# Rows of the second norm made at the head of the mix, and the norm's products run in halves

## The chip, the core and the metric

The kernel runs on one core of one Trainium2 chip. The metric is the device time of one execution in microseconds (us). TensorE (PE) does the matmuls; VectorE (DVE), ScalarE (ACT) and GpSimd (POOL) work on rows of 128 partitions; SyncE (SP) issues the DMAs, in the order of one queue. Matmul results land in PSUM, everything else lies in SBUF.

## What is computed

One layer of an encoder runs for 384 tokens: 128 sample tokens (8 sequences of 16) and 256 prompt tokens. Two branches (an RWKV-7 time mixing and a sparse attention) are projected, gated and summed, then projected once more, and a norm and a feed-forward part with many small experts (PEER) follow:

```python
mod = jax.nn.silu(c) @ lp['w_ada'] + lp['b_ada']
sh1, sc1, g1, sh2, sc2, g2 = [m[:, None, :] for m in jnp.split(mod, 6, axis=-1)]
...
m = gate_a * (o_a @ lp['w_proj_a']) + gate_b * (o_b @ lp['w_proj_b'])
x = x + g1 * (m @ lp['w_out'])
h2 = _rmsnorm(x, lp['norm2_w']) * (1 + sc2) + sh2
x = x + g2 * _peer(h2, lp['w_pq'], lp['peer_keys'], lp['peer_u'], lp['peer_v'])
```

The change touches only how `g1`, `sc2`, `sh2` and `norm2_w` are brought to the tiles, and how the line of `h2` is worked out.

## The kernel before

The tokens form three tiles of 128 rows: tile 0 the samples, tiles 1 and 2 the prompt. Matmuls split each operand into a high and a low part (`hilo`, L228: the high part on ACT, the low part on DVE or POOL) and run three products of the parts.

`run` (L1577) goes through stages. In the front the RWKV and attention units run in an order written out by hand (`ORDER`, L177), with the modulation units (`mod_unit`, L383) and the gate units between them. A modulation unit stores its 256 columns of `mod` to a DRAM buffer. Then the pools of the front are closed, the pool of the mix is opened on their memory, and `mix` (L1168) projects the two branches. `parts` (L1159) loads a branch output from DRAM in four pieces (`px`, two buffers) and splits them into `pbh`/`pbl` (first branch) or `pah`/`pal` (second). For each of eight 128-column groups it loads a gate row (`ga` in the first branch, `gm` in the second), multiplies and sums, and splits the sum into `mT`, in the buffers `pbh` and `pbl` again.

After that loop `mix` makes three sets of rows by `modrow` (L407). It loads 1024 columns of `mod` from DRAM into the one buffer `modr`, then the bias row of the same columns into its row 9 (L412, a second DMA that writes into the same tile), and multiplies by a selecting matrix, once for each of two token groups and two column halves, so that each token has its row in PSUM (`fx`, two buffers). Row 2 (`g1`) is copied by ACT to `row2`, row 4 becomes (1 + scale) x norm weight on DVE in `pah`, with the norm weights loaded into the third part of that buffer (L1191), and row 3 (the shift) is copied to `pal`. The x rows of the three tiles are loaded (L1206) into the third part of `pal` and into `ga`.

`out_unit` (L1211, four times) projects `mT` by `w_out`, multiplies by `g1` on DVE (L1219, `tm` with two buffers) and adds to the x rows on POOL (L1220). `h2_tile` (L1222, three times) stores the new x rows, squares and sums them on ACT (L1229), takes the root on POOL (L429, in `rstd`), multiplies by the root and the scale on DVE (L1231), adds the shift (L1232), and transposes on PE in two groups of four (L1241). The tile `h2` (shown as `h`) has two buffers; tile 0 also stores it to DRAM (L1234). Tile 0's transposes are split for `scores_s`, those of tiles 1 and 2 go to `h2f`, which `scores_p` and the expert matmuls read. `peer_select` (L1279) then picks the experts, mostly on DVE.

The order of instructions on each engine isn't the traced one. A scheduler lays it out before the run from a simulated time (`schedule_with_timeline_sim`, L1727): each engine takes, of what is ready in that simulation, what was traced first. On the chip each engine, and the SP queue, then follows that fixed order. A pool that takes over the memory of closed pools is a boundary: its tiles wait for the last use in those pools.

Of the kernel before, what the change touches and what calls it, by code (L numbers as in the profile page):

```python
# [17 lines left out]
AF = mybir.ActivationFunctionType  # L18
OP = mybir.AluOpType
# [176 lines left out]
class K:  # L196
    def __init__(self, ctx, tc, I, O):
        self.ctx, self.tc, self.nc, self.I, self.O = ctx, tc, tc.nc, I, O
        self.uid = 0
        self.const = self.open(ctx, "const")  # L200
        self.stream = self.open(ctx, "stream")
        self.dram = self.open(ctx, "dram", space=bass.MemoryType.DRAM)
        self.nlo = 0
        self.lo_pattern = "v"
# [55 lines left out]
    def win_ap(self, name):  # L260
        n = UNITS[name][1]
        return self.I["w_in"][:, UOFF[name]:UOFF[name] + 8 * n].rearrange("p (k c) -> p k c", k=8)

# [30 lines left out]
    def load_consts(self, n, pool):  # L294
        arr, offs = PACKS[n]
        cp = pool.tile([128, arr.shape[1]], F32, name=n)
        self.nc.sync.dma_start(cp, self.I[n])
        for k, (o, shp) in offs.items():
# [7 lines left out]
    def setup(self):  # L306
# [4 lines left out]
        cols = self.fconst.tile([128, 91], F32, name="cols")  # L311
        nc.sync.dma_start(cols, self.I["cols"])
        o = 0
# [15 lines left out]
    def setup_front(self):  # L329
# [4 lines left out]
        rn = self.t([128, 128], tag="qkn")  # L334
        nc.sync.dma_start(rn, self.I["rows"][:, 5120:5248].to_broadcast([128, 128]))
        self.load_consts("clate", self.const)
# [831 lines left out]
    def mix(self):  # L1168
        nc = self.nc
        I = self.I  # L1170
        gb = self.t([128, 8, NT], tag="ga")
        for br, (src, w, tg) in enumerate(((self.oad, "w_proj_a", "pb"), (self.obd, "w_proj_b", "pa"))):
            LT = self.parts(src, tg)
            if br:
                mh, ml = self.mT = [self.t([128, 8, NT], F32R, tag=tag) for tag in ("pbh", "pbl")]
            for u in range(4):
                W = self.wload(I[w][:, u], 256)
                for c in range(2):
                    k = 2 * u + c
                    g = self.t([128, NT], tag="gm", bufs=2) if br else gb[:, k]  # L1180
                    nc.sync.dma_start(g, self.gd[8 * br + k])
                    p = self.tposp(W, c, 128, LT)
                    nc.vector.tensor_tensor(g, g, p, op=OP.mult)
                    if br:
                        nc.gpsimd.tensor_tensor(g, g, gb[:, k], op=OP.add)
                        self.hilo(mh[:, k], ml[:, k], g, eng="v")

        self.g1 = self.t([128, 2, 1024], tag="row2")
        an = self.t([128, 3, 1024], tag="pah")
        bx = self.t([128, 3, 1024], tag="pal")  # L1190
        nc.sync.dma_start(an[:, 2], I["rows"][:, 0:1024].to_broadcast([128, 1024]))  # L1191
        self.A2, self.B2 = an, bx
        for j in (2, 4, 3):
            pp = self.modrow(j)
            for sp in range(2):
                for b in range(2):
                    cols = slice(b * 512, b * 512 + 512)
                    if j == 4:
                        nc.vector.scalar_tensor_tensor(an[:, sp, cols], pp(sp, b), 1.0, an[:, 2, cols], op0=OP.add, op1=OP.mult)
                    else:  # L1200
                        nc.scalar.activation((self.g1 if j == 2 else bx)[:, sp, cols], pp(sp, b), AF.Copy)
        self.x1 = [bx[:, 2]]
        xr = self.t([128, 2, 1024], tag="ga")
        self.x1 += [xr[:, 0], xr[:, 1]]
        for i in range(3):
            nc.sync.dma_start(self.x1[i], I["x"][i * 128:(i + 1) * 128])  # L1206
        self.x1d = self.dt_([NT, 1024])
        self.h2d = self.dt_([128, 1024])
# [13 lines left out]
    def h2_tile(self, i):  # L1222

        nc = self.nc
        x1 = self.x1[i]
        nc.sync.dma_start(self.x1d[i * 128:(i + 1) * 128], x1)
        h2 = self.t([128, 1024], tag="h2", bufs=2)
        ss = self.t([128, 1], tag="ss", bufs=2)
        nc.scalar.activation(h2, x1, AF.Square, accum_out=ss)  # L1229
        r = self.rstd(ss, ss, 1.0 / 1024, EPS)  # L1230
        nc.vector.scalar_tensor_tensor(h2, x1, r, self.A2[:, min(i, 1)], op0=OP.mult, op1=OP.mult)  # L1231
        nc.vector.tensor_tensor(h2, h2, self.B2[:, min(i, 1)], op=OP.add)  # L1232
        if i == 0:
            nc.sync.dma_start(self.h2d, h2)  # L1234
        if i == 0:
            self.h2T = [self.t([128, 8, 128], F32R, tag="poh", bufs=2, pool=self.sel) for _ in "hl"]
        t0 = max(i - 1, 0) * 128
        for hb in range(2):
            p = self.ps([128, 4, 128], tag="fx")
            for c in range(4):  # L1240
                nc.tensor.transpose(p[:, c], h2[:, (hb * 4 + c) * 128:(hb * 4 + c + 1) * 128], self.ident)  # L1241
            hs = slice(hb * 4, hb * 4 + 4)
            o = (slice(None), hs, slice(t0, t0 + 128))
            if i == 0:
                self.hilo(self.h2T[0][o], self.h2T[1][o], p, eng="v")
            else:
                nc.scalar.activation(self.h2f[o], p, AF.Copy)
# [492 lines left out]
```

## Time and profile before

| | |
|---|---|
| median of 3 runs | 1787.35 us (1784.87 to 1787.41) |
| the profiled execution's own time | 1789.7 us |
| its span | 1787.9 us |
| mean PE clock granted | 0.978 |
| PE, DVE, ACT, POOL busy | 95%, 77%, 42%, 31% |
| mean DMA rate | 244 GB/s |

The page cuts the span into 40 slices of 44.7 us; a digit is the busy share in tenths:

```profile
PE   6999999999999998999999999999998989999998
DVE  4538787777867765455999998899957877888787
DMA  9443662454364365665498989975589989999995
```

The mix and the norm lie in slices 16 to 19 (about 708 to 850 us). Times in views are microseconds from the start of the span; "idle before" in brackets is how long an engine stood still ahead of an instruction, and what ended that. Durations of single instructions come from this one execution.

### The profile page before, as it was taken

What the parts mean: (1) busy time and instruction counts of PE and PEld (TensorE: products, weight loads), DVE (VectorE), ACT (ScalarE), POOL (GpSimd) and SP (SyncE); (2) the same over time, 40 slices, a digit from 0 to 9 for tenths busy, and PEclk for the clock granted to TensorE, in tenths of its full rate; (3) what the DMA queues carried; (4) which work ended last, traced back from release to release, by engine and by line L of the source; (5) the groups of instructions that cost most, each with busy time, mean ns of one, the idle gap of its engine ahead of it and who ended that gap; (6) DMA issues with size and microseconds to landing.
All of it is one profiled execution on the core that took longest, in us unless ns stands there. A gap on an engine that the chain in (4) does not pass through costs nothing.

```text
span 1787.9 us, 33229 instructions
## 1 busy us (share of the span) xinstructions
PE 1695.1 (95%) x12424; PEld 1414.2 (79%) x12424; DVE 1368.0 (77%) x2925; ACT 754.4 (42%) x1647; POOL 556.7 (31%) x648
## 2 busy tenths in 40 slices
PE   6999999999999998999999999999998989999998
PEld 4987788878888876998788789999976666666666
DVE  4538787777867765455999998899957877888787
ACT  4533333333243333334323365579833433334344
POOL 2423243333332320034032232333342324233232
PEclk8999899999999998999999999999999999999999
DMA  9443662454364365665498989975589989999995
GB/s 319 150 121 92 195 191 73 145 166 146 95 208 141 104 219 203 202 199 176 131 349 328 347 303 375 367 239 178 186 316 369 354 332 388 388 359 372 382 371 190
DMA packets 172537, 436.71 MB, mean 244 GB/s; under 512 B 46036, under 2 KB 86100, under 8 KB 155992
## 3 DMA queue, kind: packets, MB, share of 16 engines
q1 hardware_dynamic: 153944, 300.36, 49.9%
q0 software_dynamic: 18432, 134.23, 19.8%
q8 instruction: 98, 1.61, 0.4%
q14 instruction: 63, 0.52, 0.1%
HBM read 403.23 MB, written 31.30 MB: 243 GB/s over the span
## 4 chain that ended last, share of the span: by engine, by line
PE 55%; DVE 19%; DMA 13%; issue 7%; ACT 3%; POOL 2%; SPq 1%; DVEq 0%; POOLq 0%; ACTq 0%
PE mm L226 21%; PE fx L226 13%; PE dx L226 8%; PE cp L226 6%; PE bx L226 5%; DMA w<-in_pv 4%; DVE wl L234 3%; DMA w<-in_puT 3%; DVE raw L1567 3%; DVE acc L1573 2%; DMA raw<-in_puv,pe 2%; ACT wh L230 1%; DMA d<-MBp 1%; DMA NL<-d 1%; DMA w<-in_w_ada 1%
## 5 line engine op out<-in xcount | busy, mean ns | idle before, releaser
L234 DVE TENSOR_TENSOR wl<-w,wh 128x1024 fp32r<-128x1024 f32 (+1 forms) x280 | 352.8, 1265 | 121.2 <-ACT wh L230 80.2
L230 ACT ACTIVATE wh<-w 128x1024 fp32r<-128x1024 f32 (+1 forms) x288 | 301.1, 1052 | 195.0 <-PE mm L226 83.9
L1560 POOL DMA_INDIRECT raw<-in_puv,pe x128 | 169.3, 1323 | 438.8 <-PE dx L226 128.3
L226 PE MATMUL fx<-h2h,wl 128*128 128x256 f32 x736 | 210.5, 286 | 9.5 <-DVE wl L234 9.3
L226 PE MATMUL fx<-h2h,wh 128*128 128x256 f32 x736 | 212.9, 289 | 5.0 <-ACT wh L230 3.0
L226 PE MATMUL fx<-h2l,wh 128*128 128x256 f32 x736 | 207.6, 282 | 0.0
L1573 DVE SCALAR_TENSOR_TENSOR acc<-raw,dots,acc 128x1024 f32<-128x1024 f32 x127 | 166.5, 1311 | 18.3 <-ACT dots L1569 18.1
L1567 DVE SCALAR_TENSOR_TENSOR raw<-raw,sh 128x1024 f32<-128x1024 f32 x128 | 157.8, 1233 | 9.7 <-DMA raw<-in_puv,pe 9.6
L226 PEld LDWEIGHTS fx<-h2h,wl 128*128 128x128 f32 x736 | 138.4, 188 | 13.8 <-DVE wl L234 13.4
L226 PEld LDWEIGHTS fx<-h2h,wh 128*128 128x128 f32 x736 | 138.7, 188 | 9.3 <-ACT wh L230 5.0
L226 PEld LDWEIGHTS fx<-h2l,wh 128*128 128x128 f32 x736 | 138.7, 188 | 2.1 <-issue 1.6
L226 PE MATMUL fx<-h2f,w 128*128 128x256 f32 x576 | 131.1, 388 | 8.3 <-ACT G L1476 8.3
L226 PEld LDWEIGHTS fx<-h2f,w 128*128 128x128 f32 x576 | 110.6, 194 | 27.0 <-ACT G L1476 11.1
L226 PE MATMUL mm<-LTh,wh 128*128 128x384 f32 (+2 forms) x352 | 123.8, 352 | 2.0 <-ACT wh L230 1.4
L226 PE MATMUL mm<-LTl,wh 128*128 128x384 f32 (+2 forms) x352 | 123.1, 350 | 0.9 <-POOL LTl L481 0.9
L226 PE MATMUL mm<-LTh,wl 128*128 128x384 f32 (+2 forms) x352 | 122.4, 348 | 0.0
L226 PE MATMUL mm<-wh,LTh 128*128 128x256 f32 x336 | 101.0, 301 | 2.9 <-ACT qx L881 2.9
L226 PE MATMUL mm<-wl,LTh 128*128 128x256 f32 x336 | 100.2, 298 | 0.0
L226 PE MATMUL mm<-wh,LTl 128*128 128x256 f32 x336 | 99.4, 296 | 0.0
L1568 ACT ACTIVATE dots<-dots 128x1 f32<-128x1 f32 x128 | 25.5, 199 | 155.4 <-DVE raw L1567 154.8
L1397 POOL TENSOR_TENSOR G<-G,wg 128x144 f32<-128x144 f32 (+1 forms) x64 | 54.5, 875 | 92.8 <-ACT wg L1394 89.4
L226 PEld LDWEIGHTS mm<-LTh,wh 128*128 128x128 f32 (+2 forms) x352 | 66.5, 189 | 7.8 <-issue 2.8
(559 smaller groups left out, 4204.6 us busy)
## 6 DMA issues: line engine op xcount, KB each, us to landing
w<-in_puT SPq DMA_DIRECT2D x128, 512.0 KB
w<-in_pv SPq DMA_DIRECT2D x128, 512.0 KB
w<-in_w_in SPq DMA_DIRECT2D x70, 512.0 KB
w<-in_w_ada SPq DMA_DIRECT2D x48, 512.0 KB
cKT<-in_cKT SPq DMA_DIRECT2D x32, 256.0 KB
cV<-in_cV SPq DMA_DIRECT2D x32, 256.0 KB
w<-in_w_pq SPq DMA_DIRECT2D x16, 512.0 KB
d<-wst SPq DMA_DIRECT2D x8, 832.0 KB
```

The lines of the kernel that those rows point to most:

```text
L226: return self.nc.tensor.matmul(out, l, r, start=start, stop=stop, skip_group_check=True, **kw)
L230: self.nc.scalar.activation(hi, src, AF.Copy)
L234: (self.nc.vector if eng == "v" else self.nc.gpsimd).tensor_tensor(lo, src, hi, op=OP.subtract)
L1397: (nc.vector if w is p else nc.gpsimd).tensor_tensor(g, g, w[:, :, c0:c1], op=OP.mult)
L1560: d = nc.gpsimd.indirect_dma_start(out=bass.AP(tensor=u.tensor, offset=u.offset, ap=[u.ap[0], [1, 2048]]), out_offset=None, in_=self.I["puv"],
L1567: nc.vector.scalar_tensor_tensor(u, u, 1.0, h2, op0=OP.mult, op1=OP.mult, accum_out=dot)
L1568: nc.scalar.activation(dot, dot, AF.Gelu_apprx_tanh)
L1573: nc.vector.scalar_tensor_tensor(acc, v, dot, acc, op0=OP.mult, op1=OP.add)
```

## The change

The three row sets are made first in `mix`, ahead of the branches, and nothing of the row work is left behind the loop. They lie in buffers of their own: `g1` in `row2` as before, scale in a new `row3`, shift in a new `row4`. The norm weights are loaded at the head into the buffer `pal`, which the second branch's low parts take over afterwards. The x rows of all three tiles are loaded into `pal` once the second branch is done with it, and the three h2 tiles get the buffer `pah`; the tile `h2` with its two buffers goes. In `h2_tile` the product and the shift run on two 512-column halves.

```diff
     def mix(self):
+        self.g1 = self.t([128, 2, 1024], tag="row2")
+        an = self.t([128, 2, 1024], tag="row3")
+        bx = self.t([128, 2, 1024], tag="row4")
+        rn = self.t([128, 1024], tag="pal")
+        nc.sync.dma_start(rn, I["rows"][:, 0:1024].to_broadcast([128, 1024]))
+        self.A2, self.B2 = an, bx
+        for j in (2, 4, 3):
+            pp = self.modrow(j)
+            for sp in range(2):
+                for b in range(2):
+                    cols = slice(b * 512, b * 512 + 512)
+                    if j == 4:
+                        nc.vector.scalar_tensor_tensor(an[:, sp, cols], pp(sp, b), 1.0, rn[:, cols], op0=OP.add, op1=OP.mult)
+                    else:
+                        nc.scalar.activation((self.g1 if j == 2 else bx)[:, sp, cols], pp(sp, b), AF.Copy)
         gb = self.t([128, 8, NT], tag="ga")
...
-        self.g1 = self.t([128, 2, 1024], tag="row2")
-        an = self.t([128, 3, 1024], tag="pah")
-        bx = self.t([128, 3, 1024], tag="pal")
-        nc.sync.dma_start(an[:, 2], I["rows"][:, 0:1024].to_broadcast([128, 1024]))
...
-        self.x1 = [bx[:, 2]]
-        xr = self.t([128, 2, 1024], tag="ga")
-        self.x1 += [xr[:, 0], xr[:, 1]]
+        xr = self.t([128, 3, 1024], tag="pal")
+        self.x1 = [xr[:, i] for i in range(3)]
+        self.hx = self.t([128, 3, 1024], tag="pah")
...
-        h2 = self.t([128, 1024], tag="h2", bufs=2)
+        h2 = self.hx[:, i]
...
-        nc.vector.scalar_tensor_tensor(h2, x1, r, self.A2[:, min(i, 1)], op0=OP.mult, op1=OP.mult)
-        nc.vector.tensor_tensor(h2, h2, self.B2[:, min(i, 1)], op=OP.add)
+        for hb in range(2):
+            c = slice(hb * 512, hb * 512 + 512)
+            nc.vector.scalar_tensor_tensor(h2[:, c], x1[:, c], r, self.A2[:, min(i, 1), c], op0=OP.mult, op1=OP.mult)
+            nc.vector.tensor_tensor(h2[:, c], h2[:, c], self.B2[:, min(i, 1), c], op=OP.add)
```

The removed loop over rows is the same as the added one, with the norm weights read from `an[:, 2]`. Both before and after, `mod` is complete in DRAM ahead of the mix.

More of the change, by code (lines that the diff above doesn't have):

```diff
@@ L1186, in mix @@
                         self.hilo(mh[:, k], ml[:, k], g, eng="v")
-        self.g1 = self.t([128, 2, 1024], tag="row2")
-        an = self.t([128, 3, 1024], tag="pah")
-        bx = self.t([128, 3, 1024], tag="pal")
[L1191 to L1201, printed above, removed]
-        self.x1 = [bx[:, 2]]
-        xr = self.t([128, 2, 1024], tag="ga")
-        self.x1 += [xr[:, 0], xr[:, 1]]
+        xr = self.t([128, 3, 1024], tag="pal")
+        self.x1 = [xr[:, i] for i in range(3)]
+        self.hx = self.t([128, 3, 1024], tag="pah")
         for i in range(3):
```

## The prediction

> **What bounds the kernel now.** The page comes first. It says which engine is short of time over the whole run, and nothing of one stage.
>
> ```profile
> span 1787.9 us, 33229 instructions
> PE 1695.1 (95%) x12424; PEld 1414.2 (79%) x12424; DVE 1368.0 (77%) x2925; ACT 754.4 (42%) x1647; POOL 556.7 (31%) x648
> ```
>
> TensorE (PE) is busy 95% of the span, so a change pays either by taking work off PE or by closing a hole in its time. This change takes no matmul away: it can only close holes or open new ones. The second view is therefore busy time by stretches, cut where the change acts (columns: stretch, length, then PE, PE weight loads, DVE, ACT, POOL, each with its count; PE clock, DMA share, GB/s).
>
> ```profile
> 708.00:722.00 14.00, 10.63 (x55) 8.80 (x53) 6.74 (x11) 5.90 (x12) 0.00 (x0) 0.83 0.83 292
> 789.00:796.00 7.00, 6.35 (x53) 6.15 (x51) 3.25 (x6) 1.58 (x2) 1.86 (x1) 1.00 0.89 322
> 832.00:836.00 4.00, 4.00 (x20) 3.64 (x21) 2.68 (x4) 1.92 (x3) 3.44 (x3) 0.57 0.90 279
> 846.00:848.00 2.00, 1.02 (x9) 0.81 (x8) 1.98 (x2) 0.20 (x2) 0.00 (x0) 1.00 0.91 326
> 860.00:900.00 40.00, 36.95 (x179) 29.82 (x178) 40.00 (x270) 11.79 (x21) 5.59 (x8) 0.96 0.50 158
> 900.00:1000.00 100.00, 98.01 (x462) 84.04 (x461) 97.86 (x367) 29.63 (x81) 29.11 (x24) 1.00 0.92 346
> 1000.00:1200.00 200.00, 187.18 (x1445) 180.14 (x1444) 185.62 (x282) 112.99 (x249) 65.82 (x46) 0.99 0.88 326
> 1200.00:1787.00 587.00, 558.84 (x2789) 425.63 (x2787) 467.74 (x598) 278.30 (x610) 190.40 (x178) 0.99 0.87 321
> ```
>
> The reader is to see three things. At the head of the mix (708 to 722) PE stands still for 14.00 - 10.63 = 3.37 us while DMA runs at 292 GB/s. Around the second norm (789 to 848) there are small holes and a stretch at 0.57 of the clock. And from 860 to 1000 DVE and PE are both full (40.00 of 40.00, 97.86 and 98.01 of 100): whatever the norm delivers earlier starts that stage earlier, so I let a gain at 850 pass to the end one for one.
>
> The third view is the order of time on PE, DVE, ACT and POOL around the norm, with what ended each wait in brackets.
>
> ```profile
> 789.84 0.38 SPq L1191 DMA_DIRECT2D pah<-in_rows  x1
> 795.21 1.29 DVE L1199 SCALAR_TENSOR_TENSOR pah<-fx,pah 128x512 f32<-128x512 f32 x2 [1.90 <-DMA pah<-in_rows]
> 827.77 1.28 DVE L1231 SCALAR_TENSOR_TENSOR h<-pal,ss,pah 128x1024 f32<-128x1024 f32 x1
> 828.97 1.76 DVE L234 TENSOR_TENSOR wl<-w,wh 128x1024 fp32r<-128x1024 f32 x1
> 829.86 0.28 PE L226 MATMUL mm<-wh,pbl 128*128 128x256 f32 x1
> 830.65 1.21 DVE L1232 TENSOR_TENSOR h<-h,pal 128x1024 f32<-128x1024 f32 x1
> 831.92 1.68 PE L1241 MATMUL fx<-cfirst,h 128*128 128x128 f32 x8 [1.78 <-DVE rs L425]
> 833.43 0.58 PE L226 MATMUL mm<-wh,poh 128*128 128x256 f32 x1
> 836.17 1.06 ACT L1229 ACTIVATE h<-ga 128x1024 f32<-128x1024 f32 x1 [1.95 <-DMA d<-h]
> 842.53 2.38 POOL L234 TENSOR_TENSOR wl<-w,wh 128x1024 fp32r<-128x1024 f32 x1
> 842.59 3.40 DVE L1231 SCALAR_TENSOR_TENSOR h<-ga,ss,pah 128x1024 f32<-128x1024 f32 x1 [0.44 <-POOL ss L429]
> 847.31 1.09 PE L1241 MATMUL fx<-cfirst,h 128*128 128x128 f32 x8 [0.98 <-DVE h L1232]
> ```
>
> PE ends the output projection at 829.86 + 0.28 and then waits for the first h2 tile: the product L1231, a weight split that slipped in between (828.97), and the shift L1232, which ends at 831.86. The transposes follow at 831.92. That is the clearest wait that the change touches.
>
> **The change, part by part.** Making the rows costs PE twelve row products (three rows, two group sets, two column halves).
>
> ```profile
> 736.91 0.86 PE fx L226 x2
> 765.31 0.86 PE fx L226 x2
> 805.97 1.72 PE fx L226 x4
> ```
>
> In the chain of waits each product is two passes of 0.86 us together, so twelve are 10.3 us. All stay. Before, six ran between 736 and 775 and six between 795 and 813, where PE was full in both; moved to the head, they cost the same PE time unless they fall into the 3.37 us hole. Their copies (ACT) and the scale products (DVE, 0.69 us each in the by-form view below) go along.
>
> Term a, the row of norm weights. It used to be loaded at 789.8 into the buffer of the second branch's high parts, which only then came free, and DVE waited for it until 795.21 with the residual products queued behind it. Loaded at the head into another buffer, that wait is gone: 7.00 - 6.35 = 0.65 us of PE. What is late next there is the three x rows, which now all wait for the same buffer to come free near 789; the first adder needs them only after the first projection tile, and two psum and two product buffers let PE run on. I cost that at nothing.
>
> Term b, the norm's products in halves.
>
> ```profile
> L234 DVE TENSOR_TENSOR poh<-fx,poh 128x512 fp32r<-128x512 f32 x2 | 1.4, 692 | 1.3 <-ACT poh L230 1.3
> L1199 DVE SCALAR_TENSOR_TENSOR pah<-fx,pah 128x512 f32<-128x512 f32 x4 | 2.7, 689 | 2.1 <-DMA pah<-in_rows 1.9 <-PE fx L226 0.2
> L1232 DVE TENSOR_TENSOR h<-h,pal 128x1024 f32<-128x1024 f32 x3 | 3.6, 1216 | 0.0
> ```
>
> A 512-wide product takes 0.69 us, a 1024-wide 1.22. Four halves are 2.76 us where the two whole ones are 2.50: 0.26 us more of DVE per tile. But the second product does not depend on the first shift, so DVE has something of the norm's own to do where the weight split slipped in. Started at 827.77, product, product, shift end at 829.84; the first four transposes are ready before PE's 830.14, and the other four half a microsecond later. The hole of 1.78 us closes. The split of 1.76 us then comes after the halves and ends near 832.2, ahead of the matmul that needed it at 833.4 before but only just ahead of where it is wanted now: from both sides the term lies between 0 (the split still slips in) and 1.78; I take 1.78, since the filler is there.
>
> Term c, the clock. After the hole PE ran at 0.57 for 4.00 us, which cost (1 - 0.57) x 4.00 = 1.72 us. With the hole gone it may go, but eight small transposes stay there. I take half, 0.86, with 0 and 1.72 as ends. The Trainium skill, "TensorE: Matmul & The Clock Gate", Part 1, has the array fall to half speed after an idle window of about 3.4 us that runs free of the kernel, and come back after as long a busy one. The 4 us at 0.57 agree with the way back; a hole of 1.78 us falling at all shows that a full idle window isn't needed here, and by the page's free-running window the term could be anything between its two ends.
>
> Term d, the third tile. Its square waited 1.95 us for the store of the first h2, whose buffer it shared; with three buffers that goes, and PE's 0.98 us before 847.31 with it, if nothing else is late. Next in that path are ACT and POOL's queue, so I take half, 0.49 (ends 0 and 0.98).
>
> Term e, the head.
>
> ```profile
> 707.71 0.63 PE L226 MATMUL dx<-mkp,idb 128*128 128x256 bf16 x2
> 708.41 0.80 SPq L1164 DMA_DIRECT2D px<-d  x2
> 709.26 3.27 SPq L1181 DMA_DIRECT2D ga<-d  x7
> 711.75 1.78 ACT L230 ACTIVATE pbh<-px 128x768 fp32r<-128x768 f32 x2 [1.34 <-DMA px<-d]
> 721.99 0.44 PE L226 MATMUL mm<-pbl,wh 128*128 128x384 f32 x1 [1.61 <-DVE pbl L234]
> 797.97 0.33 SPq L411 DMA_DIRECT2D modr<-d  x1
> L226 PE MATMUL mm<-pal,wh x64: 334/334/336, 753.7 to 789.1; 128*128 128x384 f32 x64
> SPq L1164 <- PE dx L226: 5.9, 1, 5.9
> SPq L412 <- DMA modr<-d: 4.7, 2, 4.0
> ```
>
> SP could not load the first branch output (px) before attention's last use of the buffers that the mix takes over (707.71 + 0.63, then 708.41). The new loads are traced ahead of px and wait for the same thing, so I expect the weight row and the first modulation row, 0.52 MB each, to stand in front of px in SP's queue. At this stretch's 292 GB/s, 1.05 MB are 3.6 us, and two issues of about 0.4 us come to it: px, ACT's split, DVE's split and PE's first branch come up to 4.4 us later. Against that, PE gets four row products (3.44 us) that it can do while it waits. The two nearly cancel; I take 0, with ends at -3.37 (products fill the hole, px not late) and +4.4. The low parts of the second branch now wait for the last scale product. Even with the two rows up to it one after another, at some 8 us to load (in the old order SP issued a row at 797.97 and its first product ran at 805.97) and 3.4 us of products each, these are done near 733, 20 us before PE used those parts (753.7).
>
> Sum: -0.65 - 1.78 - 0.86 - 0.49 + 0 = -3.8 us. Against the profiled execution's own 1789.7 (span 1787.9 and 1.8 around it) that is 1785.9; the median of the runs stands 2.35 below the profiled time, so 1787.35 - 3.8 = 1783.6. About 0.2%, 3.6 us, is what a measurement here can tell from no change, so the forecast lies just beyond it.
>
> **The rivals.** Slower: SP's queue at the head. The bias row of each modulation row must wait for the row itself to land, and the SP queue then waits with it (4.0 us at longest, above). If it is queued ahead of the third and fourth px, everything behind it on SP, px and the gate tiles, is late by that much besides the 4.4 us: 8.4 - 3.8 = +4.6, 1792. It decides if that wait comes before the last px issue, and if the row products don't refill PE. For it: DMA is the wait of this stretch already. Against: the row products are PE work that must be done anyway.
>
> No change: the third tile gates. DVE's selection needs all tiles' work ahead of it in its queue, and the third tile's path hangs on POOL's splits, not on the first tile's hole. Then only a and d are passed on: -1.1, 1786.2. For it: 842.59, where the product took 3.40 us instead of 1.28.
>
> No change, by the lock: that product began with POOL's split (842.53, 2.38) and ended 3.40 - 1.28 = 2.12 late. Cut in halves, each half can meet another POOL operation; met once more, the sum is -3.3 + 2.1 = -1.2, again 1786.2. The Trainium skill, "SBUF — State Buffer", says that DVE and GpSimd share a port pair under an exclusive lock, held for a whole instruction; this row agrees with it.
>
> Larger gain: the row products fill the hole at the head and px isn't late: -3.8 - 3.4 = -7.2, 1780.2.
>
> **How the numbers follow.** Forecast 0.30, larger gain 0.16, third tile 0.30, lock 0.05, slower 0.19. So faster 0.46, same 0.35, slower 0.19; the likeliest is 1783.6. The cases run from 1780.2 to 1792. Below, the full terms c and d (1.35 us more) lead to 1778.8, and the order of everything after 850 is laid anew by the scheduler: PE's idle time from 1000 to 1787 is 12.8 + 28.2 = 41 us, and a tenth of it, 4 us, may move either way. I give 1775 to 1792. The forecast's own range, its terms alone, is 1778.8 to 1787.
>
> **What would show it.** Right: no wait on the norm's weight row near 795; product, product, shift, shift on DVE and no PE hole over 0.5 us before the first transposes; clock near 1.00 after them; the first index search at least 3 us earlier. Term e: compare when px lands and PE's idle time from 708 to 725. Wrong: px landing 3 us late with the row products queued behind the first branch, or a stage after 860 that starts earlier but ends at the same time.

## The result, and the profile after

| | before | after |
|---|---|---|
| median of 20 runs each | 1786.06 us (1777.19 to 1792.15) | 1794.07 us (1786.68 to 1799.08) |
| ratio, after to before | | 1.0055, 95% interval 1.0041 to 1.0070 |
| profiled execution's own time | 1789.7 us | 1791.3 us |

The change makes the kernel slower by 0.55%, some 9.8 us (0.0055 x 1786; the interval is 7.3 to 12.5); the two medians themselves lie 8.0 us apart. The prediction said 3.8 us faster, with 1792 as the upper end.

The two profiles differ by only 1.7 us of span, because one execution is not the median: they stand 3.6 above and 2.7 below theirs. So two more profiles were taken, one of each kernel. The front is the same program in both, yet the mix starts anywhere from 702.8 to 714.4 us in the 18 profiles of this study. From here on, times count from the first load that SP issues for the mix. The fixed points behind it are the start of the last output matmul (`mm<-wh,pbl`) and the first and last of eight stores of `weights` (`d<-wst`). The first load, and then each fixed point's first and last start (ahead of them the durations in ns), of the kernel before in its second profile:

```profile
709.68 0.80 SPq L1164 DMA_DIRECT2D px<-d  x2
```

```profile
L226 PE MATMUL mm<-wh,pbl x96: 279/283/288, 790.0 to 830.1; 128*128 128x256 f32 x96
...
L1400 SPq DMA_DIRECT2D d<-wst x8: 319/324/327, 1163.6 to 1301.5; - x8
```

And of the kernel after, whose first load is at 702.77 (below):

```profile
L226 PE MATMUL mm<-wh,pbl x96: 278/283/283, 791.1 to 826.0; 128*128 128x256 f32 x96
...
L1403 SPq DMA_DIRECT2D d<-wst x8: 319/323/327, 1164.8 to 1302.2; - x8
```

From the mix to the last store: 1301.5 - 709.68 = 591.8 us before (595.2 in its first profile, mean 593.5), 1302.2 - 702.77 = 599.4 after (600.1 in its second). About 6 of the 9.8 us lie in this stretch. The split at the last output matmul is 120.5 + 471.4 before and 123.2 + 476.2 after: in these profiles there is a loss ahead of it and a second one behind it. The other 3 to 4 us can't be placed: what lies ahead of the mix and behind the last store differs by more than that between two executions of one program.

Now the profile after, in the order of the prediction. By stretches, at the head, after the first transposes, and in the selection:

```profile
703.60:717.60 14.00, 11.68 (x50) 10.84 (x51) 3.67 (x7) 3.19 (x9) 0.00 (x0) 0.63 1.00 321
...
827.00:831.00 4.00, 3.07 (x22) 2.54 (x23) 2.89 (x7) 2.46 (x4) 3.55 (x3) 1.00 0.80 277
...
860.00:900.00 40.00, 36.49 (x178) 29.64 (x176) 37.27 (x245) 11.12 (x23) 5.21 (x7) 1.00 0.53 182
900.00:1000.00 100.00, 95.38 (x435) 80.47 (x436) 99.86 (x381) 28.07 (x79) 27.92 (x25) 0.98 0.90 338
```

The same 14 us from the first px on, in the second profile of before, ran at 0.88 of the clock:

```profile
709.70:723.70 14.00, 11.13 (x60) 10.07 (x61) 7.28 (x11) 6.15 (x14) 0.00 (x0) 0.88 0.91 307
```

PE is as busy there as before, but at 0.63 of its clock, with DMA full; whether that clock is what costs is taken up under term e. In order of time, at the head and around the norm:

```profile
702.77 0.33 SPq L1175 DMA_DIRECT2D pal<-in_rows  x1
703.16 0.42 SPq L411 DMA_DIRECT2D modr<-d  x1
703.64 0.90 SPq L1164 DMA_DIRECT2D px<-d  x2
...
708.88 0.31 SPq L412 DMA_DIRECT2D modr<-in_b_ada  x1
709.89 1.81 ACT L230 ACTIVATE pbh<-px 128x768 fp32r<-128x768 f32 x2 [5.12 <-issue]
...
711.14 1.82 DVE L234 TENSOR_TENSOR pbl<-px,pbh 128x768 fp32r<-128x768 f32 x2
...
711.62 0.99 PE L226 MATMUL mm<-pbh,wh 128*128 128x384 f32 x2
...
713.85 0.32 SPq L1164 DMA_DIRECT2D px<-d  x1
...
717.69 1.88 PE L226 MATMUL fx<-modr,clate 128*128 128x512 f32 x4
...
823.89 1.90 DVE L1234 SCALAR_TENSOR_TENSOR pah<-pal,ss,row 128x512 f32<-128x512 f32 x2
825.71 1.21 DVE L234 TENSOR_TENSOR wl<-w,wh 128x1024 fp32r<-128x1024 f32 x1
826.85 1.28 DVE L1235 TENSOR_TENSOR pah<-pah,row 128x512 f32<-128x512 f32 x2
827.67 1.17 PE L1244 MATMUL fx<-cfirst,pah 128*128 128x128 f32 x8 [1.42 <-DVE pah L1235]
831.62 1.06 ACT L1230 ACTIVATE pah<-pal 128x1024 f32<-128x1024 f32 x1 [2.15 <-POOL pal L1221]
833.86 2.92 POOL L234 TENSOR_TENSOR wl<-w,wh 128x1024 fp32r<-128x1024 f32 x1 [2.27 <-PE mm L226]
833.86 3.47 DVE L1235 TENSOR_TENSOR pah<-pah,row 128x512 f32<-128x512 f32 x2
...
838.90 2.39 POOL L234 TENSOR_TENSOR wl<-w,wh 128x1024 fp32r<-128x1024 f32 x1
838.97 3.54 DVE L1234 SCALAR_TENSOR_TENSOR pah<-pal,ss,row 128x512 f32<-128x512 f32 x2 [0.44 <-POOL ss L429]
```

The first matmul of the first branch, in the first profile of before:

```profile
712.64 0.89 PE L226 MATMUL mm<-pbh,wh 128*128 128x384 f32 x2 [0.63 <-ACT pbh L230]
```

Four things are to be seen. The first split of px comes 6.25 us after its load was issued (703.64 to 709.89; 3.34 before), and the bias row L412 stands in SP's queue ahead of the third px, which now goes out 10.2 us after the first (713.85; 5.2 before). The branch's first matmul comes 8.9 us after the mix's first load (711.62 - 702.77; before 712.64 - 708.41 = 4.2), and the row products (`fx<-modr`) start only behind it, at 717.69. The halves did not keep the weight split out: the order is product, product, split, shift, shift, and PE still waits 1.42 us for the shift. And two halves that meet a POOL split take 3.47 and 3.54 us.

The third view is what PE waited for between the last output matmul and the first store, here of the kernel after and then of before (second profile; the line, what it waited for, us in total, times, longest):

```profile
PE fx L226 <- ACT G L1479: 8.4, 8, 1.9
PE dx L1370 <- DVE pix L1351: 3.6, 2, 3.1
...
PE fx L226 <- ACT wh L230: 1.3, 1, 1.3
```

```profile
PE fx L226 <- ACT G L1476: 7.6, 5, 3.3
PE fx L226 <- ACT wh L230: 3.5, 1, 3.5
```

The second line of after has no counterpart before. It is the transposes of the chosen indices (`pix`), which PE now meets before DVE has made them; everything behind them on PE waits too:

```profile
1024.51 0.27 PE L226 MATMUL fx<-h2l,wh 128*128 128x256 f32 x1
1027.93 0.33 PE L1370 MATMUL dx<-cfirst,pix 128*128 128x128 f32 x1 [3.15 <-DVE pix L1351]
```

No line of the change touches them. The scheduler laid out the selection anew, from simulated times that the change alters ahead of it.

### The profile page after: what moved, and what is told of

Its sections match the earlier page's. It is cut to its first block, busy times and chain, and to the rows that moved or that the text cites. A ratio compares the mean times of both kernels' runs of the same rounds, so it can differ in the third digit from the quotient of the medians.

```text
span 1789.6 us, 33231 instructions
## 1 busy us (share of the span) xinstructions
PE 1693.3 (95%) x12424; PEld 1414.1 (79%) x12424; DVE 1368.0 (76%) x2931; ACT 754.9 (42%) x1647; POOL 547.5 (31%) x648
## 5 line engine op out<-in xcount | busy, mean ns | idle before, releaser
L1563 POOL DMA_INDIRECT raw<-in_puv,pe x128 | 163.0, 1273 | 442.5 <-PE dx L226 136.8
```

What stands on the lines that cost most here:

```text
L1563: d = nc.gpsimd.indirect_dma_start(out=bass.AP(tensor=u.tensor, offset=u.offset, ap=[u.ap[0], [1, 2048]]), out_offset=None, in_=self.I["puv"],
```

## The experiments

Theory A: the rows at the head of the mix cost the time. Theory B: the scheduler's new order behind the norm costs it. Theory C: the halves cost it where they stand. All runs in one table; the ratio is from all runs of a kernel, the four columns behind it from its one profile: where the mix starts, "head" (from there to the last output matmul), "search" (first index search to last store) and "stretch" (mix to last store), all in us.

| run | what it is | ratio to before | 95% interval | mix starts | head | search | stretch |
|---|---|---|---|---|---|---|---|
| (first profile) | before | | | 708.4 | 121.4 | 450.3 | 595.2 |
| n1_before_again | before | 0.9996 | 0.9976 to 1.0016 | 709.7 | 120.5 | 447.9 | 591.8 |
| (first profile) | after | 1.0055 | 1.0041 to 1.0070 | 702.8 | 123.2 | 454.8 | 599.4 |
| e4_after_again | after | 1.0051 | 1.0030 to 1.0073 | 704.7 | 123.2 | 455.6 | 600.1 |
| e1_halves | before + halves | 1.0012 | 0.9997 to 1.0027 | 714.4 | 120.3 | 449.0 | 594.0 |
| e2_rows_whole | after, products whole | 1.0056 | 1.0040 to 1.0072 | 709.1 | 123.3 | 451.3 | 598.1 |
| e8_rows_whole_again | the same | 1.0032 | 1.0013 to 1.0052 | 705.9 | 123.2 | 450.7 | 597.4 |
| e3_rows_behind | after, rows behind the branches | 1.0029 | 1.0011 to 1.0047 | 709.1 | 125.7 | 455.2 | 602.3 |
| e5_between | after, rows between them | 1.0096 | 1.0064 to 1.0129 | 709.9 | 131.9 | 457.4 | 610.7 |
| e6_parts_first | after, px traced first | 1.0057 | 1.0033 to 1.0081 | 710.2 | 124.9 | 449.3 | 601.9 |
| e7_own_row | before + halves, own weight row | 1.0042 | 1.0019 to 1.0064 | 703.1 | 122.3 | 450.8 | 598.7 |
| f1_after_old_order | after, order of before | 1.0020 | 1.0001 to 1.0039 | 710.9 | 122.9 | 449.4 | 597.3 |
| f2_before_new_order | before, order of after | 1.0026 | 1.0005 to 1.0048 | 704.7 | 123.2 | 453.5 | 597.7 |
| f3_pe_order | after, PE's order of before | 1.0011 | 0.9994 to 1.0029 | 709.5 | 123.3 | 450.6 | 595.3 |
| g2_row_first | before, weight row loaded first | 1.0024 | 1.0000 to 1.0048 | 711.5 | 123.6 | 448.7 | 598.4 |
| g1_before_f3_order | before, order of f3 | 0.9979 | 0.9954 to 1.0004 | 711.0 | 122.3 | 448.5 | 592.1 |
| g4_g1_again | the same | 0.9987 | 0.9964 to 1.0011 | 710.4 | 123.0 | 450.1 | 594.0 |
| g3_halves_f3_order | g1 + halves | 0.9995 | 0.9970 to 1.0021 | 710.7 | 123.0 | 448.9 | 593.9 |

Roughly, the longer the stretch, the higher the ratio. The start of the mix and the time behind the last store (473.5 to 487.4 us) show no such pattern; they differ as much between two executions of one program (478.2 and 487.4 for the kernel after).

**The parts of the change, one at a time.** e1 puts only the halves into the kernel before; e2 takes only them out of the kernel after:

```diff
-            nc.vector.scalar_tensor_tensor(h2, x1, r, self.A2[:, min(i, 1)], op0=OP.mult, op1=OP.mult)
-            nc.vector.tensor_tensor(h2, h2, self.B2[:, min(i, 1)], op=OP.add)
+            for hb in range(2):
+                c = slice(hb * 512, hb * 512 + 512)
+                nc.vector.scalar_tensor_tensor(h2[:, c], x1[:, c], r, self.A2[:, min(i, 1), c], op0=OP.mult, op1=OP.mult)
+                nc.vector.tensor_tensor(h2[:, c], h2[:, c], self.B2[:, min(i, 1), c], op=OP.add)
```

> The kernel before with one edit: the second norm's two products run in halves of 512 columns; rows, buffers and the head of the mix stay as before. Order of the instructions: up to the products as before, from the first score matmuls on (selection stage, after 850 us) as in the kernel after. Theory A (the rows ahead of the branches cost it): same as before, within 3 us, so about 1786. Theory B (the halves make the scheduler lay another order for the selection stage, and that order costs it): +6 to +10 us, about 1793 to 1796, with the first index search no later than before against the first load of the mix (144.9 us) and the loss spread behind it. Theory C (the halves cost where they stand, by the lock on DVE and POOL): the first index search comes late by 2 us or more, and the total rises by that.

> The kernel after with one edit undone: the products run whole again; the rows stand at the head of the mix in buffers of their own. The order from the score matmuls on is then that of the kernel before. Theory A (the rows ahead of the branches): +6 to +10 us over before, about 1793 to 1796, with the mix 6 us longer. Theory B (the order laid anew because of the halves): the mix is 6 us longer but out_unit is shorter by as much, so the total is within 2 us of before, or up to 2 us faster: 1784 to 1788.

e1 is the same as before (1.0012), so the halves alone lose nothing that can be measured. It was expected to have the order of the kernel after, but it has a third one, so it doesn't speak against B. e2 has PE's order of before: in the traces the two agree from the last output matmul to the last store but for the name of the h2 tile. It still loses 0.56%: for A. Repeated, since the stretch was only 4.6 us longer:

> Rows at the head and whole products once more, since the first run came out 11 us slower although its stretch from the start of the mix to the last weight store was only 4 to 5 us longer. Theory A: 1790 to 1796 again. Theory B2 (its order behind the norm is that of the kernel before): the head costs 2 to 3 us and the lost halves nothing, 1784 to 1788, and the first run was an outlier.

It lost 0.32%, between both expectations, and the intervals of the two overlap. So the rows at the head, with their buffers, cost 0.3 to 0.6% by themselves.

e3 moves the rows of the kernel after behind the branches again, and keeps the rest (in the diff the block stands for its fifteen lines).

```diff
     def mix(self):
...
-        rn = self.t([128, 1024], tag="pal")
-        nc.sync.dma_start(rn, I["rows"][:, 0:1024].to_broadcast([128, 1024]))
...
         gb = self.t([128, 8, NT], tag="ga")
...
+        rn = self.t([128, 1024], tag="pal")
+        nc.sync.dma_start(rn, I["rows"][:, 0:1024].to_broadcast([128, 1024]))
...
         xr = self.t([128, 3, 1024], tag="pal")
```

> The kernel after with the rows moved back behind the two branches; own buffers and halves stay. Its order from the score matmuls on is that of the kernel after but for the last sparse rows. Theory A: no loss is left, 1783 to 1787. Theory B: the loss stays, 1791 to 1796. Theory C: the loss stays as well, and shows by the first index search.

> The kernel after once more, for a second profile and the spread: 1791 to 1796 by every theory. What of the +6.4 us between the first load of the mix and the end belongs to the program, and not to this one execution, must show again: about +1 at the end of out_unit, 0 at the first gather, +3 to +5 at the 32nd and 64th.

e3 came out at 0.29%, so something is left without the rows at the head: for B, and its search column, 455.2, is that of the kernel after. It has a flaw, since the x rows now wait for the weight row to be used up in the same buffer (`pal`), and the last output matmul starts 125.7 us after the mix, later than in any run but e5. The second profile of the kernel after repeats the first within 0.7 us up to the last store, so its loss there belongs to the program.

Next, where at the head the rows stand. e5 traces the same block between the two branches, e6 behind the first branch's `parts`; e7 is e1 with the weight row in a buffer of its own, loaded ahead of the second branch's products:

```diff
             LT = self.parts(src, tg)
+            if br == 0:
+                self.rows2()
```

> The kernel before once more, against itself: ratio 1.000 by every theory, and the interval shows what a comparison of five rounds can tell. Its profile is the second of the kernel before. Theory A (the rows ahead of the branches cost it, +2 us by the end of out_unit and more behind): the stretch from the first load of the mix to the last weight store is again 595 us within 1 us, and the clock is lost again in the stretches in which the first profile has it. What the two profiles differ by ahead of the mix and behind the last weight store is the spread between executions, some 4 us each.

> The kernel after, with the rows made between the two branches and not ahead of them; own buffers and halves stay, and the order from the score matmuls on is that of the kernel after, on the POOL queue instruction by instruction. Theory A1 (what costs is that the first branch's loads and splits stand behind the rows): the loss of the head goes, 2 to 4 us less than the kernel after, 1785 to 1788. Theory A2 (what costs is the rows' work itself, in whatever place ahead of out_unit): no gain against the kernel after, 1790 to 1795. Theory B (the order behind, laid anew because of the halves): as A2 in the total, with the loss behind the first gather.

> The kernel after, with the first branch's four loads and splits traced ahead of the rows and the rest as it is. Theory A1: the first split comes 3 to 4 us behind its load, as before (3.3), not 6.2, and the total falls by 2 to 4 us against the kernel after, to 1787 to 1790. Theory A2: as the kernel after, 1790 to 1795. The order behind 850 us is a third one here, so a difference of 3 us in either direction would also fit theory B.

> The kernel before with the halves and with the norm's weight row in a buffer of its own, loaded ahead of the second branch's products; the six row products stay behind the branches, other buffers as before. Theory A: the wait of 0.65 us for that row near 795 us goes and nothing is paid at the head, so 1782 to 1786, at or below the kernel before. Theory B: the loss of the halves' order stays, 1786 to 1792.

(The diff is that of e6; `rows2` holds the block. e5 has `if br:` ahead of `parts`.) None is a gain. e5 is the worst of all, beyond every expectation. By A1 this place should have been cheap, but it pays a price of its own, so it doesn't settle what the loads of the first branch cost. PE's waits from the mix to the last branch matmul, and what ended the idle time ahead of the second branch's splits, say why:

```profile
PE fx L226 <- DMA modr<-in_b_ada: 4.9, 1, 4.9
```

```profile
  DMA px<-d: 18.1, 3
```

The second branch's loads stand in SP's queue behind the modulation rows, each of which waits for `modr` to come free and for its bias row: PE waits 4.9 us for a bias row, and the splits of the second branch 18.1 for px. In e6 the first split comes 3.3 us after its load as expected, but the weight row and the first modulation row now stand ahead of the third px, whose split starts 13.5 us after the mix's first load instead of 10.2, and nothing is gained. That it is the transfers that cost wherever in the head they stand is argued from this, not shown: e6 has an order of its own behind the norm. e7 should have come out at or below before by A; it lost 0.42%, which is in the range of B, and why is not settled.

One transfer alone: g2 is the kernel before with the weight row loaded ahead of px, held in the old order behind the norm (how is said below).

```diff
+        rn = self.t([128, 1024], tag="row5")
+        nc.sync.dma_start(rn, I["rows"][:, 0:1024].to_broadcast([128, 1024]))
         gb = self.t([128, 8, NT], tag="ga")
...
-        nc.sync.dma_start(an[:, 2], I["rows"][:, 0:1024].to_broadcast([128, 1024]))
...
```

> The kernel before with the norm's weight row (512 KB) in a buffer of its own and loaded ahead of the first branch's loads; row products, halves and all else as before, and the order behind the norm's tiles held as before. Theory A3 (what the head pays is the transfers put ahead of the first branch's loads, the row and the first shift row, 1 MB): the first split comes 4.5 to 5 us behind its load instead of 3.3, and the end of out_unit 0.5 to 1.5 us later; total +0 to +2 us, 1783 to 1787. If only the row products' place matters (A2): no change, 1781 to 1784, less the 0.65 us wait for the row near 795 us.

```profile
711.49 0.33 SPq L1172 DMA_DIRECT2D row<-in_rows  x1
711.88 0.90 SPq L1164 DMA_DIRECT2D px<-d  x2
717.12 1.76 ACT L230 ACTIVATE pbh<-px 128x768 fp32r<-128x768 f32 x2 [3.62 <-issue]
```

717.12 - 711.88 = 5.24 us, against 3.3 without the row and 6.25 with the row and a modulation row ahead. That is a little above A3's 4.5 to 5. The ratio, 1.0024, is above the 0 to 2 us that A3 gave, and its interval touches 1.0000: it leans the same way but doesn't prove a loss.

**The order alone.** In these runs each engine's instructions behind the norm's tiles are tied into a chain, in an order read from another kernel's program. The ties fix the order only and wait for nothing. `TAIL` lists the positions.

```diff
+        traced = list(self.nc.cur_bb.bb.instructions)
+        tail = traced[[i.name for i in traced].index(mark.name) + 1:]
+        for order in zlib.decompress(base64.b85decode(TAIL)).decode().split(";"):
+            q = [tail[int(n)] for n in order.split(",")]
+            for x, y in zip(q, q[1:]):
+                self.tc.add_manual_dep(y, x.name, mybir.DependencyInfo(
+                    mybir.DependencyClass.NoSync, mybir.DependencyReason.DATA), reason="order")
```

> The kernel after, complete, with one thing fixed: from the end of the second norm's tiles on, each engine's instructions are held in the order in which the kernel before has them. Theory B2 (the loss behind the first index search is the order that the scheduler laid for the selection and the dense blocks, and it follows from the change only through the plan): the stretch from the first index search to the last weight store falls from 455 us to 448 to 450 us, and the total to within 3 us of the kernel before, 1783 to 1788. Theory A (rows ahead of the branches): as the kernel after, 1790 to 1795, and the stretch stays at 455 us.

> The kernel before, with rows, buffers and whole products as they were, held from the end of the second norm's tiles on in the order of the kernel after. Theory B2: it loses what the change lost behind the index search without any part of the change itself: the stretch from the first index search to the last weight store rises from 449 us to 454 to 456 us, the total by 4 to 7 us to 1787 to 1790. Theory A: as the kernel before, 1781 to 1785.

> The kernel after with the order of the kernel before held on TensorE alone, behind the second norm's tiles; the scheduler lays the other engines anew. If what costs is that TensorE stands behind transposes of the selection that wait for VectorE (B2, TensorE's part): the 455 us fall to 448 to 451, total 1783 to 1788. If it is VectorE's order: 453 us or more, total 1789 to 1795. Theory A: 1790 to 1795.

The stretch from the first index search to the last store is 450.3 and 447.9 us in the two profiles of before, 454.8 and 455.6 after. The complete change in the old order has 449.4, and its ratio falls from 1.0051 and 1.0055 to 1.0020; PE's old order alone is enough for 450.6 and 1.0011. The kernel before in the new order has 453.5 and loses 0.26%, without one line of the change. All three totals came out in the ranges that B2 gave, or within 1 us of them (f1 stands 3.6 us above before by its ratio, where B2 said 3), and the stretches too but for f2's, which is 0.5 us short of 454 to 456. The wait goes with the order, too. PE's waits for `pix` and `wh` from the last output matmul to the first store, in f2 and then in f3:

```profile
PE dx L1367 <- DVE pix L1348: 3.8, 2, 3.3
...
PE fx L226 <- ACT wh L230: 1.5, 2, 1.3
```

```profile
PE fx L226 <- ACT wh L230: 3.5, 1, 3.5
```

So the new order costs something by itself, about half of the loss by whole runs: f2 says 4.6 us (0.0026 x 1785, interval 0.9 to 8.6), the difference from the kernel after to f1 0.31 to 0.35%, some 6 us. Single profiles show less. The new order takes 4 to 6 us more from the first index search to the last store, but starts that search 2 to 4 us earlier; from the last output matmul to the last store f2 takes 474.5 us (before 473.7 and 471.4), and f1 474.4 (after 476.2 and 476.9), some 2 us either way. f2's long head, 123.2, lies ahead of the held order and isn't part of this. Nor is it all the one wait: the wait for `wh` that the new order saves, 2.2 us against the second profile of before (0.5 against the first), has to be set against the 3.6. The rest is spread over the selection's interleaving with the dense blocks and was not pinned to a line.

**The halves in one order, and a best version.** g1 is the kernel before in f3's order, g3 the same with halves, g4 g1 again:

> The kernel before, rows, buffers and whole products as they were, held behind the second norm's tiles in the order of the run with TensorE's old order (TensorE as in the kernel before, the other engines as laid anew there). By the milestones it should take the head of the kernel before (121 us from the start of the mix to the end of out_unit) and the 472 us of that run behind it, 593 us to the last weight store: 1781 to 1785, the same as the kernel before within what is measurable. If VectorE's order were a gain of its own, the first index search stays 2 us earlier and the total falls to 1779 to 1781.

> The kernel before with the halves alone, in the same held order as the first run of this call: the difference of the two is the halves and nothing else. If the halves save what they were credited with (b and c, 2.6 us, by closing the hole ahead of the second norm's transposes): 2 to 3 us less than that run. If they give nothing: the same within 2 us. If they cost 1.5 us, as the run with all of the change in the old order suggests between out_unit and the first gather: 1 to 2 us more.

> The first run of the call before once more: the kernel before in the held order, which came out at 0.9979 of the kernel before with an interval that takes in 1. If that order is a gain on the kernel before: 0.997 to 0.999 again, 1779 to 1782. If the kernel before and this are the same program in time, which the milestones say (592.2 us from the start of the mix to the last weight store, against 591.9 and 595.2): 0.999 to 1.001, 1783 to 1786.

g3 stands 0.08 and 0.16% above g4 and g1, within their intervals: no saving is seen, though 2.6 us is too little for these intervals to exclude. The profiles lean the other way, for the first index search comes 22.0 us after the last output matmul in g3 and 21.3 and 20.9 in g1 and g4. That is less than the 2 us of theory C. g1 and g4 are 0.21 and 0.13% below before, both with intervals that take in 1. A version that beats the kernel before is not shown; this is the nearest to one.

## Why the prediction was wrong

**Term a** (-0.65, the wait for the weight row) was right in its mechanism and too large. That wait is gone. But the seven microseconds at the same place, counted from the first output matmul (791.1 instead of 789.6), still have a hole:

```profile
790.47:797.47 7.00, 6.60 (x54) 6.40 (x53) 3.23 (x6) 1.58 (x2) 2.11 (x2) 1.00 0.87 326
```

PE waits 0.40 us there for the first residual product on DVE (`tm`, L1220). The prediction had looked for what comes late next at the x rows, and costed it at nothing; 0.25 us of the gain is left. The price of the earlier load was booked in term e, at nothing.

**Term b** (-1.78, the hole before the transposes) failed. It said that product, product, shift would follow each other since the filler was there. The scheduler put the weight split between products and shifts again, and PE waited 1.42 us: near the lower end, 0, with 0.36 us gained. The index search did start 2.1 us earlier after the last output matmul (847.3 - 826.0 = 21.3 against 853.6 - 830.1 = 23.5), but not because of the halves: whole products in the new order have 21.0 (f2), halves in the old order 24.9 (f1).

**Term c** (-0.86, the clock at 0.57) rested on one execution. In the second profile of before the 4 us around the same transposes ran at full clock:

```profile
833.20:837.20 4.00, 3.35 (x26) 3.05 (x26) 3.43 (x4) 1.61 (x3) 2.53 (x3) 1.00 0.89 315
```

There was nothing sure to gain there, and that the clock is full there after the change isn't shown to be the change's doing. Why the same hole cost its clock in one execution and not in the other is told in the last section.

**Term d** (-0.49): the wait for the store of the first h2 is gone (831.62 waits for POOL alone). What came late next is what the lock rival described: the third tile's products met a POOL split and took 3.54 us for two halves, where 0.69 us a half had been reckoned. The second tile's shifts met one as well (3.47; 1.21 before). The Trainium skill, "SBUF — State Buffer", section "Who interferes with whom", with its exclusive lock on the port pair of DVE and GpSimd, agrees with these rows. In all, PE waits 3.8 us for the three tiles, where it waited 2.8 and 3.2 in the two profiles of before: b and d together, -2.27 in the sum, came out as a small loss.

**Term e** (0, the head) is the first step that decided. "The two nearly cancel" was wrong, and on the side of the row products. The late px was sized about right: up to 4.4 us were reckoned, and the branch's first matmul comes 8.9 us after the mix's first load instead of 4.2 and 4.4 (8.1 to 8.9 in all six profiles with the rows first). But the row products weren't there to fill that time. In PE's fixed order they stand behind the branch's first matmuls (717.69), which is the sign of being wrong that the prediction named; until the branch began, PE did the end of attention. The condition of the slower rival came about in part. The bias row stood ahead of the third px, but that px couldn't go out before DVE had split the first one, near 712.1, so the queue held it for 1.8 us at most.

The last output matmul came 1.8 to 2.7 us later than in the two profiles of before (123.2 against 121.4 and 120.5). Even that is partly luck: f2, g1 and g4 go through the mix in the order of before, and their heads are 122.3 to 123.2. With px first, a low clock goes with a long head: the 14 us from the first px on ran at 0.88 in n1 and e1 (heads 120.5 and 120.3) and at 0.76 in f2, g1 and g4. With the rows first it makes no difference. The kernel after lost (1 - 0.63) x 14.00 = 5.2 us of clock there, n1 1.7, and e2 no more than n1:

```profile
709.99:723.99 14.00, 10.02 (x51) 8.79 (x52) 3.86 (x8) 3.23 (x8) 0.00 (x0) 0.88 0.93 309
```

Yet e2's head is as long, 123.3: PE is busy for less of the time, and waits 1.9 us for the splits of px instead. So with the rows first it is the late loads and not the clock that set the end of the head, as far as these six profiles show. By whole runs the rows at the head cost 0.2 to 0.56% (f1, e8, e2), 3.6 to 10 us, more than the 2 us that the head shows; where the rest arises is open.

**The step that was missing** is the order. The text said that "the order of everything after 850 is laid anew by the scheduler" and allowed it 4 us either way, but had no term or rival for it, and counted on a gain at 850 passing to the end one for one. The 4 us went into the lower end alone (1778.8 - 4 gives 1775); the upper end, 1792, is the slower rival without them. The new order gave 2 us at the index search and took some 6 behind it (455.2 against 449.1, means of two profiles). By whole runs, some 5 to 6 us for the order (f2, f1) and about as much for the rows at the head (f1, e8, e2) make the 9.8; the intervals of each are wide.

Of the rivals, the slower one had the right sign and the right queue, and its 1792 came nearest. But it took the whole 8.4 us from SP's queue, where the head ended at most 2.7 us later, and knew nothing of the order: that its number came near is luck.

## What to carry to other kernels

Where a scheduler lays out the order from simulated times, any edit is two changes, the edit and a new order for everything behind it; hold the old order, or put the new order on the old kernel, before believing either a gain or a loss. A load moved to the head of a stage that waits for DMA delays the loads behind it, and work that is meant to fill the wait helps only if the fixed order puts it there. Before a hole or a dip in the clock is priced, look at a second execution.

## What the runs showed of the hardware

The clock at the head fell without a long hole. In all 18 profiles PE's clock is either full or half, and a spell of either, but for those cut off at the ends, lasts a whole multiple of 3.41 us. Here is the kernel after in such pieces, cut where its clock changes (PE clock is the third number from the end), and then PE's longest waits in the first three:

```profile
701.93:705.35 3.42, 1.50 (x10) 0.87 (x8) 2.23 (x6) 2.04 (x8) 0.00 (x0) 1.00 0.46 117
705.35:708.76 3.41, 2.66 (x12) 2.26 (x12) 0.69 (x1) 0.00 (x0) 0.00 (x0) 0.50 0.96 264
708.76:712.17 3.41, 2.86 (x12) 2.63 (x13) 1.37 (x3) 1.85 (x3) 0.00 (x0) 0.50 1.05 398
712.17:715.59 3.42, 3.42 (x12) 3.42 (x11) 0.79 (x1) 0.23 (x1) 0.00 (x0) 0.50 1.06 342
715.59:719.00 3.41, 3.41 (x17) 2.67 (x16) 1.11 (x1) 1.28 (x2) 0.00 (x0) 1.00 0.97 320
```

```profile
PE dx L1085 <- ACT se L1077: 1.0, 1, 1.0
PE dx L226 <- DVE asum L1093: 0.9, 1, 0.9
```

As far as the profile's busy time tells, PE was busy for 44% of the piece ahead of the fall (1.50 of 3.42 us) and never waited longer than 1.0 us. It stayed at half clock through two pieces with 2.66 and 2.86 us of work, and came back after one without a hole. The Trainium skill, "TensorE: Matmul & The Clock Gate", Part 1, gives an idle window of about 3.4 us as the condition. The length agrees with these rows; but the window ahead of the fall was not idle, so if the rule asks for one without work, the measurement stands against it here.

Where a hole lies in these pieces seems to decide, too, as far as one pair of executions tells. The hole of 1.78 us before the norm's transposes lies within one piece in the first profile of before, and the clock is at half in the next; in the second profile it falls across two, and the clock stays full:

```profile
828.85:832.27 3.42, 1.64 (x14) 1.44 (x14) 3.40 (x5) 2.59 (x4) 1.21 (x2) 1.00 0.56 178
```

```profile
828.18:831.59 3.41, 2.24 (x19) 2.04 (x17) 3.41 (x3) 1.63 (x3) 1.75 (x1) 1.00 0.35 145
831.59:835.00 3.41, 2.15 (x14) 1.71 (x15) 2.24 (x5) 2.39 (x4) 2.86 (x2) 1.00 0.93 322
```

The same front took from 702.8 to 714.4 us in 18 executions. That spread alone is larger than the effect under study.
